# Twelve unread float32 products between the first modulation rows, and the first scores two steps of the key stream later

## The chip, the cores and the metric

One core of a Trainium2 chip runs the whole program. The metric is its time on the device in microseconds (us). The engines are named as in the profile: PE (TensorE, products), PEld (its weight loads), DVE (VectorE), ACT (ScalarE), POOL (GpSimd) and SP (SyncE, which here only issues transfers). Each engine works through its own instructions in a fixed order and waits on semaphores of the others.

## The reference

One inference step of a diffusion trunk of two layers on 512 latent tokens (a grid of 8 rows by 64 columns) and 128 prompt tokens, model width 1024, 16 heads of 64. Layer 0 is neighbourhood attention, layer 1 grouped-query attention; behind each stands a gated FFN with a width-3 convolution.

```
for l in range(2):
    shift, scale, gate (x2) = split(silu(cond) @ ada_w[l] + ada_b[l], 6)   # for latents and for prompt
    h = rmsnorm(x, g_pre[l]) * (1 + scale) + shift
    q, k, v = h @ w_qkv[l]
    x = x + gate * rmsnorm(attention(q, k, v, cached k, cached v) @ w_o[l], g_post[l])
    h = rmsnorm(x, g_ffn_pre[l]) * (1 + scale') + shift'
    u = conv3(h @ w_up[l]) + conv_b[l];  a, b = split(u, 2)
    x = x + gate' * rmsnorm((silu(a) * b) @ w_down[l], g_ffn_post[l])
```

Outputs are both token groups and the prompt's new keys and values.

## The kernel before, in words

Weights come as float32 and are split into a high part (`wh`, a cast on ACT) and the rest (`wl`, a subtraction on POOL or DVE); activations likewise. A large product is then three passes: high by high, low by high, high by low. All products are issued through `mm` and transposes through `turn`, which chain them so that PE runs them exactly in the order in which the program is written. The other engines' orders are set by a scheduler that models when things are ready; its order is fixed when the program is built, and each engine then runs its own in sequence. A transfer on SP's queue also waits its turn behind the one ahead.

*Start.* The tokens are loaded, normalised and transposed into `xT` (`tr`). For each of four pairs of 128-wide slices of the model width, `mod_load(i)` fetches four tiles `wf` of `ada_w` (seven buffers) and `mod_rows(i)` multiplies them with the conditioning vectors: for each tile four products of 32 output rows, which fill the four quarters of one bank named `row`. ACT copies the bank to `rs` (one buffer). `mod_cols(i)` turns it with four products by `sel`, two columns wide (`col`), and DVE and ACT then form the high and low part of `hT` for the two slices. The program order on PE is: rows 0, rows 1, columns 0, rows 2, columns 1, the value products `vp` of slices 0 and 1 for two token tiles (twelve), columns 2, the other `vp` of slices 0 and 1 and all of slices 2 and 3 (48), rows 3, and so on. `vb` holds five banks for the values of the five token tiles; each uses its columns 0 to 255.

*Attention of layer 0.* `stream()` yields the projections as 173 steps of six (keys and queries, `qk`) or up to nine products (values, `vp`): for each of eight pairs of heads eight steps for the queries and eight for the keys, and between them the values of heads 4 to 15. A step at the end of a half evicts its bank (`qs`; `kh` and `kl`), certain steps also issue the next weights' loads and splits, and the last item's steps 0, 2 and 4 issue those of the output projection (`m0.weights`, on POOL). `PRO` steps are drawn before the first head's scores:

```
        for _ in range(PRO):
            fill(1, 0)
        head = Head(0)
        for slot in range(4):
            head.scores(slot)
            fill()
```

Each of the four scores (`s`) is followed by a further step. Then come the heads: the letters of `ORDER` say what stands between the turns (`t`, which transpose the probabilities `p` into `tp`) of one head and the scores of the next: `f` draws a step, `a` a piece of `ada_work`, the later modulation rows (`ada`). The softmax of a score runs through DVE (minimum), ACT (exponential), DVE (reciprocal) and POOL (`p`); POOL also makes each head's table `tb` of biases from `tr`, which ACT's queue loads. With 19 steps ahead, 23 are drawn when head 0's loop begins and 165 when head 12's does; head 12 draws the last eight, and what it would draw beyond them is nothing. Then the weights and heads' outputs are split (`oh`, `ol`) and the output projection (`y`) starts.

*FFN.* `ux`, `uy`, `uz` are its up-products; on SP's queue loads of `in_ffn_w_up`, loads of `in_ada_w` for `ada_work`, stores of activations (`act`) and their reloads (`ain`) stand in one order.

Of the kernel before, what the change touches and what calls it, by code (L numbers as in the profile page):

```python
# [53 lines left out]
    "t0 s0 s1 f a f a f f t1 f f t2 a a f a f f a a s2 a f f a s3 f f a f f".split(),  # L54
    "t0 p0 s0 s1 f a f a f f t1 t2 a a f a f f a a v s2 p1 a f a s3 f p2 f".split(),
)
PRO = 19
PSTEP = (3, 5, 6, 6, 8, 9)
WU = 29
TP = 1  # L60
# [41 lines left out]
def hybrid_step(ctx: ExitStack, tc: tile.TileContext, A, O):  # L102
# [4 lines left out]
    def pe(ins):  # L107

        if pe_last[0] is not None:
            tc.add_manual_dep(ins.ins, pe_last[0], no_sync, reason="order")  # L110
        pe_last[0] = ins.ins.name

    def mm(*a, **k):
        pe(nc.tensor.matmul(*a, **k))  # L114
# [21 lines left out]
    ident = cst.tile([P, P], F32, name="ident")  # L136
# [317 lines left out]
    with ExitStack() as s:  # L454
# [3 lines left out]
        xts = []  # L458
# [51 lines left out]
        def mod_rows(i, ws):  # L510


            row = bk.get("row")
            for (n, h), w in ws.items():
                for j in range(4):
                    k = 4 * h + j
                    mm(row[32 * j : 32 * j + 32, 256 * n : 256 * n + 256], scolp[:, 2 * k : 2 * k + 32],
                       w[:, j, :], start=h == 0, stop=h == 1)
            rs = sp.tile([P, 512], F32, tag="rs", name="rs")
            nc.scalar.copy(rs, row)  # L520
            bk.put(row)
            return rs
# [41 lines left out]
        vb = [bk.get("vp") for _ in range(NT)]  # L564
# [13 lines left out]
        for t in range(NT):  # L578
            x_turn(t)
        rs = mod_rows(0, loads[0])  # L580
        for i in range(1, 3):
            nxt = mod_rows(i, loads[i])
            mod_cols(i - 1, rs)
            rs = nxt
        v_part(0, (0, 1))
        mod_cols(2, rs)
        v_part(0, (2, 3, 4))
        v_part(1, range(NT))
        rs = mod_rows(3, loads[3])
        v_part(2, (0, 1, 2))  # L590
        mod_cols(3, rs)
# [99 lines left out]
    with l_na:  # L691
# [261 lines left out]
        def fill(n=1, a=2):  # L953
            for _ in range(n):
                next(work, None)
            for _ in range(a):
                next(ada0, None)

        for _ in range(PRO):
            fill(1, 0)  # L960
# [620 lines left out]
    for hq in range(2):  # L1581
        for n, t in enumerate(((4, 0, 1, 2, 3), (0, 1, 2, 3, 4))[hq]):
# [3 lines left out]
            i = 5 * hq + n  # L1586
# [221 lines left out]
```

## Time and profile before

| | us |
|---|---|
| median of three runs | 1630.63 |
| lowest and highest | 1628.24, 1637.93 |
| the profiled execution's own time | 1631.72 |
| its span, first to last instruction | 1629.9 |
| PE busy in it | 1557.0 |

The mean granted clock of PE over the span is 0.986. In the profile a line such as `26.72 0.64 PE L114 MATMUL row<-wf,scolp 128*32 128x256 f32 x8 [0.87 <-DMA wf<-in_ada_w]` reads: at 26.72 us, lasting 0.64, eight records of products into `row` from `wf` and `scolp`, issued at line 114 (the helper `mm`; 117 is `turn`), before which PE sat idle for 0.87 until the load of `wf` landed. One float32 product leaves two records. Weights split into two parts leave one record for each product.

### The profile page before, as it was taken

Reading aid. Unit: us, or ns where it says so; the run is one execution under the profiler, and the core shown is the slowest. Engines: PE = TensorE matmul, PEld = TensorE weight load, DVE = VectorE, ACT = ScalarE, POOL = GpSimd, SP = SyncE. Lnnn points to the kernel's source line nnn. Section 1 sums busy time; section 2 is a strip of 40 time slices with the busy share of each in tenths; the row PEclk is TensorE's granted clock in tenths of the full one; section 3 lists DMA queues with packets and bytes.
Section 4 is the critical chain, followed back from the end, with each engine's and each line's share of the span. In section 5 each row is a group of like instructions: output and inputs, shape, how many; then the busy total and the mean of one; then the engine's idle time right before and its main releaser. Section 6 shows DMA issues by size and latency. Waiting matters only on the chain.

```text
span 1629.9 us, 26039 instructions
## 1 busy us (share of the span) xinstructions
PE 1557.0 (96%) x9709; PEld 1350.8 (83%) x9709; DVE 1011.8 (62%) x1645; ACT 858.0 (53%) x1641; POOL 723.0 (44%) x614
## 2 busy tenths in 40 slices
PE   5999999899999999999999997999999999999998
PEld 3888889778888888998887776777898999998886
DVE  3453534549866565775465877773787888885454
ACT  3464646545545454554444445763565656565433
POOL 1554545423253544544343355441524556563333
PEclk8999999999999999999999999999999999999999
DMA  9745553245466666348575110002635333338664
GB/s 286 184 138 143 137 143 73 63 135 176 147 199 214 196 204 207 103 161 299 197 235 178 60 39 14 1 1 101 220 114 187 117 103 109 107 115 285 209 210 140
DMA packets 193211, 242.42 MB, mean 149 GB/s; under 512 B 11100, under 2 KB 149564, under 8 KB 193084
## 3 DMA queue, kind: packets, MB, share of 16 engines
q1 hardware_dynamic: 182224, 233.13, 45.2%
q10 hardware_dynamic: 10860, 7.62, 2.7%
q8 instruction: 76, 1.25, 0.3%
q14 instruction: 51, 0.42, 0.1%
HBM read 214.38 MB, written 26.34 MB: 148 GB/s over the span
## 4 chain that ended last, share of the span: by engine, by line
PE 65%; DVE 12%; POOL 6%; DMA 6%; issue 5%; ACT 4%; SPq 1%; ACTq 0%; POOLq 0%; DVEq 0%
PE acc L114 18%; PE ux L114 10%; PE y L114 7%; PE qk L114 5%; PE uz L114 5%; PE s L114 4%; PE po L114 4%; PE tp L117 3%; PE vp L114 3%; DMA wr<-in_ada_w 3%; PE uy L114 3%; POOL wl L1099 2%; PE ada L114 2%; DVE t L1175 2%; DVE al L1099 1%
## 5 line engine op out<-in xcount | busy, mean ns | idle before, releaser
L167 POOL TENSOR_TENSOR wl<-wr,wh 128x1024 fp32r<-128x1024 f32 x75 | 183.7, 2452 | 267.1 <-ACT wh L165 260.6
L1099 POOL TENSOR_TENSOR wl<-wr,wh 128x1024 fp32r<-128x1024 f32 x80 | 194.6, 2451 | 55.5 <-ACT wh L1098 46.2
L114 PE MATMUL ux<-B,wh 128*128 128x322 f32 x832 | 201.9, 313 | 1.7 <-DVE B L220 1.6
L1175 DVE SCALAR_TENSOR_TENSOR t<-C,cw,t 128x644 f32<-128x644 f32 x176 | 156.5, 889 | 57.4 <-ACT t L1173 56.6
L114 PE MATMUL acc<-wh,alo 128*128 128x512 f32 x440 | 172.0, 391 | 0.0
L114 PE MATMUL acc<-wh,ahi 128*128 128x512 f32 x440 | 171.9, 391 | 0.0
L114 PE MATMUL acc<-wl,ahi 128*128 128x512 f32 x440 | 171.8, 391 | 0.0
L165 ACT CAST wh<-wr 128x1024 fp32r<-128x1024 f32 x140 | 145.3, 1048 | 32.9 <-DMA wr<-in_ffn_w_down 23.9
L114 PE MATMUL uz<-B,wh 128*128 128x322 f32 x640 | 158.5, 316 | 0.0
L114 PEld LDWEIGHTS ux<-B,wh 128*128 128x128 f32 x832 | 143.7, 189 | 9.4 <-issue 2.9
L1068 DVE TENSOR_TENSOR alo<-ain,ahi 128x384 fp32r<-128x384 f32 (+1 forms) x88 | 70.9, 815 | 95.7 <-ACT ahi L1066 95.4
L114 PE MATMUL ux<-B,wl 128*128 128x322 f32 x416 | 129.1, 310 | 0.0
L114 PE MATMUL qk<-hT,wh 128*128 128x384 f32 (+1 forms) x512 | 126.0, 319 | 0.3 <-DVE qs L776 0.2
L114 PEld LDWEIGHTS uz<-B,wh 128*128 128x128 f32 x640 | 111.8, 190 | 6.6 <-issue 3.7
L1099 POOL TENSOR_TENSOR vl<-wr,vh 128x1024 fp32r<-128x1024 f32 x38 | 96.8, 2547 | 36.4 <-ACT vh L1098 36.4
L1098 ACT CAST wh<-wr 128x1024 fp32r<-128x1024 f32 x88 | 89.6, 1050 | 33.1 <-DVE wr L1122 31.8
L1066 ACT CAST ahi<-ain 128x384 fp32r<-128x384 f32 (+1 forms) x88 | 40.2, 461 | 124.8 <-PE acc L114 91.7
L1173 ACT ACTIVATE t<-C,cw 128x644 f32<-128x644 f32 x88 | 78.7, 895 | 48.5 <-DVE C L1203 44.3
L114 PE MATMUL uz<-B,wl 128*128 128x322 f32 x320 | 100.2, 313 | 0.5 <-POOL wl L1099 0.4
L167 DVE TENSOR_TENSOR wl<-wr,wh 128x1024 fp32r<-128x1024 f32 x65 | 83.5, 1299 | 25.0 <-ACT wh L165 24.5
L114 PEld LDWEIGHTS acc<-wl,ahi 128*128 128x128 f32 x440 | 82.6, 188 | 18.0
L114 PEld LDWEIGHTS acc<-wh,ahi 128*128 128x128 f32 x440 | 82.6, 188 | 17.7
(249 smaller groups left out, 4009.4 us busy)
## 6 DMA issues: line engine op xcount, KB each, us to landing
wr<-in_ffn_w_up SPq DMA_DIRECT2D x88, 512.0 KB
wr<-in_ffn_w_down SPq DMA_DIRECT2D x88, 512.0 KB
wr<-in_ada_w SPq DMA_DIRECT2D x80, 512.0 KB
act<-act SPq DMA_DIRECT2D x44, 321.0 KB
wr<-in_na_w_qkv SPq DMA_DIRECT2D x24, 512.0 KB
mod<-modrow SPq DMA_DIRECT2D x20, 512.0 KB
ain<-act SPq DMA_DIRECT2D x44, 192.0 KB
wf<-in_ada_w SPq DMA_DIRECT2D x16, 512.0 KB
```

The source lines that it names most:

```text
L114: pe(nc.tensor.matmul(*a, **k))
L117: pe(nc.tensor.transpose(*a, **k))
L165: i = nc.scalar.copy(hi, raw)
L167: j = (low or nc.vector).tensor_sub(lo, raw, f32(hi))
L1066: nc.scalar.copy(hi[:, 0 : c1 - c0], ain[:, 0 : c1 - c0])
L1068: nc.vector.tensor_sub(lo[:, 0 : c1 - c0], ain[:, 0 : c1 - c0], f32(hi[:, 0 : c1 - c0]))
L1098: nc.scalar.copy(hl[0], src)
L1099: low.tensor_sub(hl[1], src, f32(hl[0]))
L1173: nc.scalar.activation(t, taps(0), AF.Identity, bias=cw[:, 3, n : n + 1], scale=cw[:, 1, n : n + 1])
L1175: nc.vector.scalar_tensor_tensor(t, taps(d), cw[:, w, n : n + 1], t, op0=ALU.mult, op1=ALU.add)
```

## The change

It does two things. In `mod_rows` for rows 0, 1 and 2 each tile's four products are followed by one float32 product of the identity with 256 columns of the first token tile, into columns 256 to 511 of the last value bank, which nothing reads. And `PRO` is 21: two more steps of the stream stand ahead of the first scores, and so all later steps stand two earlier against the heads; head 12 is left with six.

```
--- before.py
+++ after.py
@@ -54,7 +54,7 @@
     "t0 s0 s1 f a f a f f t1 f f t2 a a f a f f a a s2 a f f a s3 f f a f f".split(),
     "t0 p0 s0 s1 f a f a f f t1 t2 a a f a f f a a v s2 p1 a f a s3 f p2 f".split(),
 )
-PRO = 19
+PRO = 21
 PSTEP = (3, 5, 6, 6, 8, 9)
 WU = 29
 TP = 1
@@ -510,12 +510,15 @@
         def mod_rows(i, ws):
 
 
+
             row = bk.get("row")
             for (n, h), w in ws.items():
                 for j in range(4):
                     k = 4 * h + j
                     mm(row[32 * j : 32 * j + 32, 256 * n : 256 * n + 256], scolp[:, 2 * k : 2 * k + 32],
                        w[:, j, :], start=h == 0, stop=h == 1)
+                if i < 3:
+                    mm(vb[4][:, 256:512], ident, xts[0][:, 0:256], start=True, stop=True)
             rs = sp.tile([P, 512], F32, tag="rs", name="rs")
             nc.scalar.copy(rs, row)
             bk.put(row)
```

With the written order the scheduler's order changes too. On PE, around the first score of head 0 (`s`; `qk` are the stream's products, `tk` turns the prompt's keys of the first pair), before:

```order
L114 MATMUL qk<-hT_128,wh 128x256
L114 MATMUL s<-kh_740,qs_668 128x384
L114 MATMUL s<-kl_615,qs_668 128x384
L114 MATMUL qk<-hT_127,wh 128x256
L114 MATMUL qk<-hT_127,wl 128x256
L114 MATMUL qk<-hT_128,wh 128x256
L114 MATMUL qk<-hT_127,wh 128x256
L114 MATMUL qk<-hT_127,wl 128x256
L114 MATMUL qk<-hT_128,wh 128x256
L114 MATMUL s<-kh_740,qs_668 128x384
L114 MATMUL s<-kl_615,qs_668 128x384
L114 MATMUL qk<-hT_127,wh 128x384
```

and now:

```order
L114 MATMUL qk<-hT_127,wh 128x256
L114 MATMUL qk<-hT_127,wl 128x256
L114 MATMUL qk<-hT_128,wh 128x256
L114 MATMUL qk<-hT_127,wh 128x384
L114 MATMUL qk<-hT_127,wl 128x384
L114 MATMUL qk<-hT_128,wh 128x384
L114 MATMUL qk<-hT_127,wh 128x384
L114 MATMUL qk<-hT_127,wl 128x384
L114 MATMUL qk<-hT_128,wh 128x384
L117 MATMUL tk<-ident,kp 128x128
L114 MATMUL s<-kh_752,qs_680 128x384
L114 MATMUL s<-kl_627,qs_680 128x384
```

A step of 256 columns and one of 384, with the turn behind it, have come to stand ahead of the first score instead of behind the first and the second.

On POOL, at the end of the stream in head 12 (`p` are the softmax's last steps, `wl` splits of the output projection's weights, `tb` tables), before:

```order
L167 TENSOR_TENSOR wl<-wr,wh 128x1024
L826 TENSOR_TENSOR tb_611<-mask,tr 128x2x128
L869 TENSOR_SCALAR p<-p,rc 128x384 x2
L826 TENSOR_TENSOR tb_611<-mask,tr 128x256 x2
L869 TENSOR_SCALAR p<-p,rc 128x384 x2
L826 TENSOR_TENSOR tb_612<-mask,tr 128x2x128
L869 TENSOR_SCALAR p<-p,rc 128x384
L167 TENSOR_TENSOR wl<-wr,wh 128x1024
L869 TENSOR_SCALAR p<-p,rc 128x384
L167 TENSOR_TENSOR wl<-wr,wh 128x1024
L826 TENSOR_TENSOR tb_612<-mask,tr 128x256 x2
L869 TENSOR_SCALAR p<-p,rc 128x384 x2
```

and now:

```order
L872 TENSOR_SCALAR p<-p,rc 128x384 x2
L829 TENSOR_TENSOR tb_623<-mask,tr 128x2x128
L872 TENSOR_SCALAR p<-p,rc 128x384 x2
L829 TENSOR_TENSOR tb_623<-mask,tr 128x256 x2
L872 TENSOR_SCALAR p<-p,rc 128x384 x2
L829 TENSOR_TENSOR tb_624<-mask,tr 128x2x128
L167 TENSOR_TENSOR wl<-wr,wh 128x1024 x2
L872 TENSOR_SCALAR p<-p,rc 128x384
L167 TENSOR_TENSOR wl<-wr,wh 128x1024
L872 TENSOR_SCALAR p<-p,rc 128x384
L829 TENSOR_TENSOR tb_624<-mask,tr 128x256 x2
L872 TENSOR_SCALAR p<-p,rc 128x384 x2
```

The split of the first row before has moved behind the tables and the pairs of `p`, next to the following split: three splits now stand around the two single `p`, where two did. The same two `p` end both lists.

On SP, in the first steps of the FFN of layer 0, before:

```order
L1090 DMA wr<-in_ffn_w_up 128x8x128
L1214 DMA act_0_4379<-act 128x642
L277 DMA wr<-in_ada_w 128x1024
L1090 DMA wr<-in_ffn_w_up 128x8x128
L277 DMA wr<-in_ada_w 128x1024
L1064 DMA ain<-act_0_4379 128x384
L1214 DMA act_1_4380<-act 128x642
L277 DMA wr<-in_ada_w 128x1024
L1064 DMA ain<-act_1_4380 128x384
L277 DMA wr<-in_ada_w 128x1024 x2
```

and now:

```order
L1093 DMA wr<-in_ffn_w_up 128x8x128 x2
L277 DMA wr<-in_ada_w 128x1024 x2
L1217 DMA act_0_4391<-act 128x642
L277 DMA wr<-in_ada_w 128x1024
L1067 DMA ain<-act_0_4391 128x384
L277 DMA wr<-in_ada_w 128x1024
L1217 DMA act_1_4392<-act 128x642
L1093 DMA wr<-in_ffn_w_up 128x8x128
L277 DMA wr<-in_ada_w 128x1024
L1093 DMA wr<-in_ffn_w_up 128x8x128
```

Two loads of `in_ffn_w_up` and two of `in_ada_w` now go ahead of the first store of activations; before it was one of the former alone. After some 25 transfers both orders are the same again, and from there on to the end on every engine.

More of the change, by code (lines that the diff above doesn't have):

```diff
@@ L56 @@
 )
-PRO = 19
+PRO = 21
 PSTEP = (3, 5, 6, 6, 8, 9)
@@ L518, in mod_rows @@
                        w[:, j, :], start=h == 0, stop=h == 1)
+                if i < 3:
+                    mm(vb[4][:, 256:512], ident, xts[0][:, 0:256], start=True, stop=True)
             rs = sp.tile([P, 512], F32, tag="rs", name="rs")
```

## The prediction

> **What bounds the kernel now.** I read the page first, then TensorE's waits, then the stretches that the change touches.
>
> ```profile
> span 1629.9 us, 26039 instructions
> PE 1557.0 (96%) x9709; PEld 1350.8 (83%) x9709; DVE 1011.8 (62%) x1645; ACT 858.0 (53%) x1641; POOL 723.0 (44%) x614
> PE 65%; DVE 12%; POOL 6%; DMA 6%; issue 5%; ACT 4%; SPq 1%; ACTq 0%; POOLq 0%; DVEq 0%
> ```
>
> PE is busy for 96% of the span and holds 65% of the chain that ended last. Twelve more products can only cost what no wait hides, and moving two steps of the key stream removes no work. All that is to be won is idle time (1629.9 - 1557.0 = 73 us in all) and time at a lower clock. The waits say how little of that lies in reach:
>
> ```profile
> PE ada L114 <- DMA wr<-in_ada_w: 11.9, 6, 3.3
> PE row L114 <- DMA wf<-in_ada_w: 5.9, 7, 2.7
> PE tp L117 <- POOL p L869: 3.8, 1, 3.8
> PE s L114 <- ACT kh L749: 1.6, 1, 1.6
> ```
>
> The columns are total, times, longest. `row` (the modulation rows) and `s` (the first scores) are the places edited, `tp` and `ada` are further along the streams that move. Together they are 23 us, 1.4% of the span.
>
> The clock is the other part. This is the view of busy time by stretches, cut at the places where the granted clock changes (stretch, its length, busy of PE, PEld, DVE, ACT, POOL, then PEclk, DMA share and GB/s):
>
> ```profile
> 23.22:26.64 3.42, 2.34 (x40) 0.88 (x32) 0.00 (x0) 0.58 (x1) 0.00 (x0) 1.00 1.09 348
> 26.64:30.05 3.41, 2.26 (x24) 1.28 (x24) 0.16 (x2) 0.10 (x1) 0.00 (x0) 1.00 1.10 349
> 30.05:33.46 3.41, 0.88 (x8) 0.23 (x8) 1.60 (x5) 3.41 (x6) 1.21 (x1) 0.50 1.09 347
> 33.46:36.88 3.42, 2.36 (x20) 0.41 (x16) 3.35 (x5) 0.20 (x1) 1.15 (x1) 0.50 1.09 348
> 36.88:40.29 3.41, 3.29 (x18) 2.48 (x19) 0.60 (x4) 0.32 (x1) 0.00 (x0) 0.50 1.09 348
> 40.29:43.70 3.41, 3.41 (x19) 3.41 (x17) 0.55 (x1) 3.40 (x6) 1.41 (x1) 0.50 1.13 333
> 43.70:47.12 3.42, 3.42 (x17) 3.42 (x17) 2.90 (x9) 2.43 (x5) 0.94 (x1) 0.50 1.21 291
> 47.12:50.53 3.41, 3.41 (x31) 3.41 (x30) 3.41 (x5) 1.86 (x2) 2.53 (x1) 1.00 1.21 258
> 81.25:84.66 3.41, 1.62 (x10) 1.19 (x10) 1.51 (x4) 3.30 (x8) 0.54 (x1) 1.00 0.75 176
> 84.66:88.08 3.42, 3.42 (x14) 3.32 (x13) 1.44 (x5) 3.29 (x8) 2.66 (x2) 0.50 0.07 20
> ```
>
> The clock is 0.50 from 30.05 to 47.12 and again from 84.66 to 88.08. It falls behind a stretch with 1.62 us of work and behind one with 2.26, but not behind one with 2.34. It comes back behind a stretch full of wide products (43.70), not behind 2.36 us of work (33.46), nor behind the two stretches from 36.88 that look full. These contain `col`, products that move two columns only: 1.87 and 1.25 us of it, and 1.05 us in the stretch at 26.64. So `col` seems to count for little as activity.
>
> **Edit 1, the twelve products.** The rows around them, from the timeline of PE:
>
> ```profile
> 21.96 2.96 PE L114 MATMUL row<-wf,scolp 128*32 128x256 f32 x40
> 25.21 0.64 PE L114 MATMUL row<-wf,scolp 128*32 128x256 f32 x8 [0.29 <-DMA wf<-in_ada_w]
> ...
> 28.23 0.64 PE L114 MATMUL row<-wf,scolp 128*32 128x256 f32 x8 [0.88 <-DMA wf<-in_ada_w]
> 28.80 1.05 PE L114 MATMUL col<-sel,rs 128*128 128x2 f32 x8
> 32.58 1.08 PE L114 MATMUL row<-wf,scolp 128*32 128x256 f32 x8 [2.72 <-DMA wf<-in_ada_w]
> ...
> 37.00 1.08 PE L114 MATMUL row<-wf,scolp 128*32 128x256 f32 x8 [0.43 <-DMA wf<-in_ada_w]
> 38.01 1.87 PE L114 MATMUL col<-sel,rs 128*128 128x2 f32 x8
> ...
> 42.45 1.70 PE L114 MATMUL col<-sel,rs 128*128 128x2 f32 x8
> ...
> 51.24 1.93 PE L114 MATMUL row<-wf,scolp 128*32 128x256 f32 x32
> ```
>
> Eight records are one group of four `row` products on one loaded tile. No row shows a float32 product of 128 by 128 with 256 columns, so I bound it. Four groups back to back take 1.93 at full clock and one alone 0.64, so a group in a row takes (1.93 - 0.64) / 3 = 0.43. The four of a group write four quarters of the partitions, the new product all of them at once, with as many columns: 0.43 is the nearest row. From below, four `col` products with a full stationary tile take 1.05, 0.26 each; from above, a group alone, 0.64. Twelve cost 3.1 to 7.7 us, 5.2 by the value taken. At half clock I double it to 0.86.
>
> The cover is the 5.9 us that `row` waits for its loads. Rows 0 and 1: five products stand ahead of the second group of row 1, so PE gets there at 24.92 + 5 x 0.43 = 27.1, its load long landed, and three groups and products of 0.86 end at 29.6, not 28.87. The first `col` comes 0.8 later, inside the 2.72 that PE waits until 32.58 anyway; the loads are a stream at 348 GB/s that does not hurry. Row 2: its loads land 1.47 us apart ((37.00 - 32.58) / 3). At full clock group and product take 0.86 and fit; `col` starts at 37.00 + 0.86 = 37.9, as before (38.01). At half clock they take 1.72, and do not fit: with the first pair ending at 33.4 at full clock, the others run 33.99, 35.7, 37.4 to 39.1, and `col` starts 1.1 later.
>
> So the sign hangs on the clock. With the products, the stretch from 26.64 is full but for `col`, so I expect 1.00 up to 33.46. The stretch from 30.05 then holds 0.9 us of them and the end of `col`, less than the 1.62 that lost the clock at 84.66, so it falls at 33.46. The next stretch holds work from 33.99 on, 2.89 us. The trace has 2.36 as too little and 3.42 as enough; 2.89 lies half way. I take it as enough, narrowly: the added products fill the whole array, unlike `col`. Then 1.00 returns at 36.88 instead of 47.12. `col` takes 1.05 for 1.87 (-0.8), the twelve value products up to 42.45 half of their 2.6 (-1.3), the next `col` 1.05 for 1.70, of which I count 0.5: **-2.6 us**, and the vector work behind starts as much earlier. I go no further, since DVE is busy for all of 47.12 to 50.53. If 2.89 is not enough, the next stretch holds 39.1 - 36.9 = 2.3 and the one after that 2.6 besides `col`, which is less, and all stays slow until 47.12: the 1.1 above, rounded to **+1.2 us**. Bounds: -4.6 (all of PE's work from 38.01 to 47.12 at double speed) to +2.5 (three products of row 2 at the upper price, 1.28 for 0.86, on top of 1.2).
>
> The Trainium skill, "TensorE: Matmul & The Clock Gate", Part 1, says that the clock opens after at least one busy window of about 3.4 us of sustained work and closes after an idle one. The trace agrees on the length (3.41) and on opening behind a full stretch, but not on closing: 2.26 busy of 3.41 lost it. By the page's word "sustained", 2.89 would not open it, and the sum would be that of the first rival below.
>
> **Edit 2, the first scores two steps later.**
>
> ```profile
> 77.41 0.52 PE L114 MATMUL qk<-hT,wh 128*128 128x384 f32 x2
> ...
> 78.47 0.52 PE L114 MATMUL qk<-hT,wh 128*128 128x384 f32 x2
> ...
> 80.12 0.40 PE L114 MATMUL qk<-hT,wh 128*128 128x256 f32 x2
> ...
> 80.83 0.40 PE L114 MATMUL qk<-hT,wh 128*128 128x256 f32 x2
> 83.03 0.44 PE L114 MATMUL s<-kh,qs 128*128 128x384 f32 x1 [1.56 <-ACT kh L749]
> 83.70 0.41 PE L114 MATMUL s<-kl,qs 128*128 128x384 f32 x1 [0.23 <-DVE kl L750]
> ```
>
> Six products of a step take 0.71 (80.83 - 80.12) or 1.06 (78.47 - 77.41). One step of each now stands ahead of the first score: 1.8 us of work against 1.56 + 0.23 of waiting. The keys' parts come when they came, so I leave 0.4 of waiting for the low part: -1.4. With the gap gone, the stretch from 81.25 is nearly full and the clock should stay at 1.00: half of 3.42, -1.7. Against it: the softmax of the first head now has two steps less behind it before its turns, and the turn waits for the last `p`:
>
> ```profile
> 91.81 1.15 POOL L869 TENSOR_SCALAR p<-p,rc 128x384 f32<-128x384 f32 x2
> ...
> 93.09 0.60 PE L117 MATMUL tp<-ident,p 128*128 128x128 f32 x4
> ```
>
> `p` ends at 92.96, 0.13 ahead of the turn, so there is no slack. The moved steps also put their own work ahead of that softmax: four evictions of `qs` on ACT and DVE, and behind the turn of `kp` a copy and a store on ACT's queue. Their loads were issued before step 19 and do not move against the scores. I take +0.5. Sum **-2.6**, bounds -3.5 (all of gap and clock) to +0.5 (the 1.8 comes back in front of the turn with the slow stretch behind it, so that nothing is won, and the 0.5 is lost).
>
> **What is late next: the end of the stream.** The two steps are missing in head 12, which draws 6 steps instead of 8.
>
> ```profile
> 302.45 2.39 POOL L167 TENSOR_TENSOR wl<-wr,wh 128x1024 fp32r<-128x1024 f32 x1
> ...
> 306.56 2.35 POOL L167 TENSOR_TENSOR wl<-wr,wh 128x1024 fp32r<-128x1024 f32 x1 [1.16 <-ACT wh L165]
> ...
> 310.50 1.16 POOL L869 TENSOR_SCALAR p<-p,rc 128x384 f32<-128x384 f32 x2
> ```
>
> Here PE's only long wait of this phase ends: 3.8 in the waits, `tp` for `p`. POOL works off two splits (`wl`), a table and `p`; in the new order three splits stand there, one more at 2.4. PE arrives with 1.8 us less work behind the scores of the next head. At worst both add up, +4.2; if ACT's and POOL's work starts as much earlier as the steps do, nothing, or -0.5. POOL idles in places before it, so I take half: **+2.0**. SyncE's queue is reordered in the first steps of the next phase, the conv FFN: `ada_w` loads pass activation stores. PE waits there for them:
>
> ```profile
> 441.23 0.64 PE L114 MATMUL ada<-wr,scolp 128*32 128x256 f32 x8 [1.12 <-DMA wr<-in_ada_w]
> ...
> 462.87 0.64 PE L114 MATMUL ada<-wr,scolp 128*32 128x256 f32 x8 [1.76 <-DMA wr<-in_ada_w]
> ```
>
> and, from the view by stretches, the one behind the second wait:
>
> ```profile
> 463.53:466.94 3.41, 3.41 (x13) 3.41 (x14) 1.72 (x4) 1.58 (x3) 1.75 (x1) 0.50 0.63 155
> ```
>
> If both waits and the slow stretch behind the second go: -1.1 - 1.8 - 1.7 = -4.6. If a load now comes later, the longest such wait, 3.3, with a slow stretch: +5.0. I see no reason for a side and take 0. The order of what follows that phase's first steps is unchanged on every engine.
>
> **Sum.** The profiled execution took 1631.72 (span 1629.9). -2.6 - 2.6 + 2.0 + 0 = -3.2: **1628.5 us**. That execution is 1.1 above the median of the runs (1630.63; 1628.24 to 1637.93), less than they scatter; I do not correct for it.
>
> **The rivals.**
> - *The products do not open the clock* and only delay row 2. For it: 2.89 is unproven, the trace fails at 2.36. +1.2 for -2.6: 1631.72 + 1.2 - 2.6 + 2.0 = 1632.3. This is also what the change comes to if it doesn't do what it says. The Trainium skill's sentence on a sustained window, named above, gives this one.
> - *Slower: POOL's queue in head 12.* The third split comes straight ahead of the first `p` of head 13 and the filler is gone: +4.2, and one more stretch at half clock behind the longer wait, +1.7, together 5.9 for the 2.0 taken. It decides once this sum passes the gains: 5.2 with the forecast's clock (1631.72 - 5.2 + 5.9 = 1632.4), 1.4 with the first rival's (1636.2). I put it half way, 1634.3. For it: the new order of POOL's rows. Against it: POOL is busy for only 44% of the span, so its work can slide ahead.
> - *SyncE's order decides*: both `ada` waits go (1628.5 - 4.6 = 1623.9) or one of 3.3 comes (1633.5).
>
> **Chances and range.** Forecast 0.45, first rival 0.32, slower 0.15, SyncE 0.08. Range 1622 to 1637: the forecast without the +2.0 and with the `ada` waits gone is 1622, the slower case with a scatter of 1 is 1637. About 1% (16 us) is what a measurement of this kernel can tell from no change; no case comes near it. I leave 0.02 for faster and 0.03 for slower, 0.95 for within 1%.
>
> **What would show it.** Clock 1.00 up to 33.46 and from 36.88 on; PE's wait for `wf` down from 5.9 to under 3; no wait of `s` over 0.5 near 80 and no 0.50 behind it; the wait of `tp` for `p` near 305 grown from 3.8 to about 6; `ada` waits of similar sum. The forecast is wrong if the clock stays at 0.50 until 47, if that wait passes 7, or if the first turns wait for `p` by what the scores no longer wait.

## The result, and the profile after

The changed kernel took 1644.59 us (median of five runs, 1642.11 to 1645.37), the kernel before 1630.63 (the median of five as well) in the same session. The ratio is 1.0072 with a 95% interval of 1.0048 to 1.0095; it is an estimate over all the runs, and the two medians alone would give 1.0086. The change is slower by 0.7%, where 1628.5 was forecast and 1637 was the upper end. The profiled execution is the 1644.59 itself. Its page (the span, the busy time by engine):

```profile
span 1642.6 us, 26081 instructions
PE 1564.3 (95%) x9733; PEld 1353.4 (82%) x9733; DVE 1018.1 (62%) x1645; ACT 859.4 (52%) x1641; POOL 725.2 (44%) x614
```

PE is busy 7.3 us longer (1564.3 for 1557.0), and the rest of the 12.7 us of span is idle time. Its waits (total, times, longest):

```profile
PE tp L117 <- POOL p L872: 10.9, 4, 3.9
...
PE ada L114 <- DMA wr<-in_ada_w: 7.8, 5, 2.4
...
PE tp L117 <- DVE qs L779: 5.5, 3, 1.8
...
PE vp L114 <- DVE hT L547: 4.5, 4, 1.3
...
PE s L114 <- DVE qs L779: 2.1, 3, 0.8
...
PE row L114 <- DMA wf<-in_ada_w: 0.8, 1, 0.8
```

The edited waits are gone: `row` for `wf` is down from 5.9 to 0.8, and `s` for `kh` is no longer in the list. Four others have grown or are new. Where the loss stands can be read from the busy time up to the first product of the output projection (`y`, at 315.0 before and 333.7 after), first before and then after:

```profile
0.00:315.00 315.00, 288.96 (x2130) 249.99 (x2131) 134.03 (x362) 173.91 (x442) 148.90 (x158) 0.96 0.56 149
```

```profile
0.00:333.74 333.74, 295.05 (x2154) 251.73 (x2155) 141.42 (x366) 175.46 (x446) 151.98 (x158) 0.95 0.52 142
```

PE's idle time up to there grew from 26.0 to 38.7, by 12.7, and its busy time by 6.1, through the added products and through work at half clock. So at `y` the kernel is 18.7 late, more than at its end (12.7). Nearly all of the added idle time falls into six places:

| place | before | after | |
|---|---|---|---|
| `row` for `wf` | 5.9 | 0.8 | -5.1 |
| first scores | 1.8 | 0 | -1.8 |
| value products for `hT` | 2.1 | 4.5 | +2.4 |
| first turn of head 0 for `p` | 0 | 3.4 | +3.4 |
| heads 1, 5, 9 for `qs` | 0 | 7.6 | +7.6 |
| end of the stream | 4.2 | 9.7 | +5.5 |
| sum | | | +12.0 of 12.7 |

**The start.** The stretches of the changed kernel, cut where its granted clock changes (columns as in the forecast):

```profile
30.47:33.89 3.42, 2.47 (x27) 1.44 (x25) 0.91 (x4) 2.44 (x4) 0.14 (x1) 0.99 1.10 349
33.89:37.30 3.41, 3.41 (x20) 1.21 (x12) 3.16 (x3) 1.27 (x3) 2.21 (x1) 0.51 1.09 348
37.30:40.71 3.41, 3.41 (x31) 2.74 (x30) 1.64 (x6) 1.06 (x2) 0.00 (x0) 1.00 1.09 348
...
44.13:47.55 3.42, 0.94 (x6) 0.52 (x5) 3.39 (x8) 3.12 (x5) 0.24 (x1) 0.99 1.20 291
47.55:50.96 3.41, 3.41 (x16) 3.41 (x17) 3.41 (x4) 1.16 (x2) 3.23 (x1) 0.51 1.14 291
...
98.75:102.16 3.41, 3.41 (x21) 2.57 (x20) 2.20 (x8) 2.82 (x10) 0.62 (x2) 0.51 0.58 171
```

The clock does what was forecast: 1.00 to 33.89, one slow stretch, 1.00 again from 37.30 and not from 47.12. But the gain does not get past the vector work. PE, DVE and POOL around 42, in three fences:

```profile
40.93 0.95 PE L114 MATMUL col<-sel,rs 128*128 128x2 f32 x8
...
45.57 0.51 PE L114 MATMUL vp<-wh,hT 128*128 128x256 f32 x2 [1.21 <-DVE hT L547]
...
47.47 0.80 PE L114 MATMUL vp<-wh,hT 128*128 128x256 f32 x2 [1.28 <-DVE hT L547]
```

```profile
41.92 0.16 DVE L538 SCALAR_TENSOR_TENSOR gcol<-col,colb 128x4 f32<-128x4 f32 x1 [0.39 <-PE col L114]
42.00 0.15 DVE L540 TENSOR_TENSOR hcol<-col,colb 128x4 f32<-128x4 f32 x1
42.12 2.28 DVE L539 TENSOR_TENSOR gcol<-gcol,colb 128x4 f32<-128x4 f32 x1
44.32 0.34 DVE L546 TENSOR_SCALAR xT<-xT,gcol,hcol 128x128 f32<-128x128 f32 x1
```

```profile
41.96 2.41 POOL L167 TENSOR_TENSOR wl<-wr,wh 128x1024 fp32r<-128x1024 f32 x1 [5.86 <-ACT wh L165]
```

`col` comes at 40.93 instead of 42.45 and runs at full clock, so DVE's first `gcol`, which reads it, stands at 41.92 instead of 44.19, 2.3 earlier. The second `gcol`, four columns wide, then lasts 2.28 and ends at 44.40, when POOL's split ends (41.96 + 2.41 = 44.37). In the kernel before, the split ran from 42.29 to 44.64, and `gcol` came at its end:

```profile
44.38 0.27 DVE L536 TENSOR_TENSOR gcol<-gcol,colb 128x4 f32<-128x4 f32 x1
```

So the vector work behind it starts at 44.32 for 44.58: of 2.3 us, 0.3 are left, PE waits twice for `hT`, and behind a stretch with 0.94 of work the clock is 0.50 again from 47.55.

**The first turn.** The turn of head 0 waits for the last `p` (first PE, then POOL):

```profile
98.04 0.33 PE L117 MATMUL tp<-ident,p 128*128 128x128 f32 x1 [3.35 <-POOL p L872]
```

```profile
95.08 2.35 POOL L167 TENSOR_TENSOR wl<-wr,wh 128x1024 fp32r<-128x1024 f32 x1
97.40 0.59 POOL L872 TENSOR_SCALAR p<-p,rc 128x384 f32<-128x384 f32 x1
```

In the new order a split of weights stands ahead of that `p`; before, the split followed it (`p` from 91.81, `wl` at 94.64). The wait is twice what the scores saved, and the slow stretch has moved with it, from 84.66 to 98.75.

**Heads 1, 5 and 9.** In these heads the prompt's scores (`sp`) are issued. PE, and DVE's queue beside it, in head 1:

```profile
119.50 0.44 PE L114 MATMUL s<-kh,qs 128*128 128x384 f32 x1 [0.75 <-DVE qs L779]
...
123.00 0.63 PE L117 MATMUL tp<-ident,p 128*128 128x128 f32 x4 [1.82 <-DVE qs L779]
```

```profile
118.06 1.38 DVE L779 SCALAR_TENSOR_TENSOR qs<-qk,qs 64x256 fp32r<-64x256 f32 x3 [6.07 <-ACT qs L778]
119.47 0.42 DVE L627 TENSOR_REDUCE nmp<-sp 128x2 f32<-128x256 f32 x1
119.93 0.56 DVE L779 SCALAR_TENSOR_TENSOR qs<-qk,qs 64x384 fp32r<-64x384 f32 x1
120.52 0.42 DVE L627 TENSOR_REDUCE nmp<-sp 128x2 f32<-128x256 f32 x1
...
122.63 0.23 DVE L779 SCALAR_TENSOR_TENSOR qs<-qk,qs 64x64 fp32r<-64x64 f32 x1
```

A turn reads no `qs`: what it waits for is the bank, which the eviction of the queries has yet to empty. With the stream two steps further, that eviction stands among the prompt's reductions (`nmp`) and the next head's minimum in DVE's order, and its last piece ends at 122.86. Heads 5 and 9 show the same two waits (0.81 and 1.82, 0.55 and 1.82): 7.6 in all.

**The end of the stream** (PE's three long waits, two of the stretches there, then POOL and DVE):

```profile
320.15 0.33 PE L117 MATMUL tk<-ident,kp 128*128 128x128 f32 x1 [2.14 <-ACT kp L793]
324.93 0.48 PE L117 MATMUL tp<-ident,p 128*128 128x128 f32 x1 [2.97 <-POOL p L872]
329.33 0.47 PE L117 MATMUL tp<-ident,p 128*128 128x128 f32 x1 [3.92 <-POOL p L872]
```

```profile
317.20:320.61 3.41, 1.27 (x8) 0.94 (x7) 1.54 (x5) 3.36 (x10) 3.41 (x2) 0.99 0.14 47
320.61:324.03 3.42, 1.35 (x5) 0.66 (x3) 2.95 (x6) 3.08 (x8) 3.42 (x4) 0.50 0.75 262
```

```profile
316.18 4.68 POOL L167 TENSOR_TENSOR wl<-wr,wh 128x1024 fp32r<-128x1024 f32 x2
...
327.06 3.33 POOL L872 TENSOR_SCALAR p<-p,rc 128x384 f32<-128x384 f32 x2
```

```profile
326.30 1.87 DVE L167 TENSOR_TENSOR wl<-wr,wh 128x1024 fp32r<-128x1024 f32 x1
328.09 1.85 DVE L915 TENSOR_TENSOR ol<-of,oh 128x640 fp32r<-128x640 f32 x2
```

One wait of 3.8 and a short one have become four, 9.7 together with a last one of 0.65, and the clock is 0.50 for 17.1 us (five stretches from 320.61) instead of 6.8. Two splits now run one after the other ahead of the first of the last four `p`, and a third behind it. And the last two `p` take 3.33, where two took 1.16 in the kernel before (310.50 in the forecast's rows), while DVE works on a split and on `ol`: that is some 2.2 of the 5.5 that this place lost.

**Behind it** the kernel makes good 6.0 of the 18.7 us, 4.3 of them up to the first of the last products (`acc`) of the FFN of layer 0. Among PE's waits there, those of `ada` are shorter. Whose doing that is, the experiments below ask and do not settle.

### The profile page after: what moved, and what is told of

It is laid out like the page before. It is cut to its first block, busy times and chain, and to the rows that moved or that the text cites. A ratio compares the mean times of both kernels' runs of the same rounds, so it can differ in the third digit from the quotient of the medians.

```text
span 1642.6 us, 26081 instructions
## 1 busy us (share of the span) xinstructions
PE 1564.3 (95%) x9733; PEld 1353.4 (82%) x9733; DVE 1018.1 (62%) x1645; ACT 859.4 (52%) x1641; POOL 725.2 (44%) x614
## 4 chain that ended last, share of the span: by engine, by line
PE 72%; DVE 9%; POOL 6%; DMA 4%; ACT 4%; issue 4%; ACTq 0%; SPq 0%; POOLq 0%; DVEq 0%
PE acc L114 18%; PE ux L114 12%; PE y L114 7%; PE qk L114 6%; PE uz L114 5%; PE po L114 4%; PE s L114 4%; PE vp L114 4%; PE tp L117 3%; PE uy L114 3%; POOL wl L1102 2%; PE ada L114 2%; DMA wr<-in_ada_w 2%; PE gp L114 2%; DVE al L1102 1%
```

## The experiments

The first four rows separate the parts. The ratio is to the kernel before, run on the same chip in the same session. The changed kernel and the two steps alone ran five times, one step and the last splits on DVE four times, the moved prompt's scores six times, the others ten or twelve times; the intervals are as wide as that makes them.

| kernel | median us | ratio (95%) |
|---|---|---|
| changed kernel | 1644.59 | 1.0072 (1.0048 to 1.0095) |
| products alone | 1632.17 | 0.9994 (0.9975 to 1.0012) |
| two steps alone | 1647.81 | 1.0081 (1.0052 to 1.0110) |
| first two scores alone | 1627.12 | 0.9969 (0.9952 to 0.9985) |
| one step | 1649.19 | 1.0092 (1.0063 to 1.0122) |
| two steps, prompt's scores moved | 1638.61 | 1.0052 (1.0034 to 1.0070) |
| two steps, given back in head 11 | 1639.47 | 1.0044 (1.0025 to 1.0064) |
| two steps, last splits on DVE | 1643.60 | 1.0082 (1.0051 to 1.0114) |
| two steps, both mends | 1632.27 | 1.0016 (1.0001 to 1.0032) |
| products, one split on DVE | 1631.93 | 1.0007 (0.9994 to 1.0021) |
| first two scores and products | 1627.38 | 0.9975 (0.9958 to 0.9991) |
| the same, one split on DVE | 1627.76 | 0.9972 (0.9957 to 0.9988) |
| one product ahead of head 0 | 1629.37 | 0.9988 (0.9970 to 1.0006) |
| the same, first two scores | 1627.94 | 0.9979 (0.9963 to 0.9996) |

**Products alone** (the lines in `mod_rows`, `PRO = 19`).

> The twelve unread products alone, the stream drawn as before (PRO = 19). My theory after the first comparison: the products do bring the clock back near 37, but what PE gains up to 43 it then waits for the vector work behind hT, and falls to half clock again, so that at the first product of the stream it stands about where it did in the changed kernel (+3.2 us against before), while everything behind costs what it did before: 1631 to 1635 us. Rival A (the products are what makes the changed kernel slow, through a clock history that goes on into the later stages): 1640 or more. Rival B (the forecast's own sum for this part, -2.6): about 1628.

It is no change that can be told from noise: 0.9994. The interval goes down to 0.9975, so the time alone doesn't exclude the forecast's -2.6 either. At the first product of the stream it stands +0.58 against before, not +3.2 as the theory had it; the changed kernel's profiled execution had two further slow stretches from 61.20. Kernels that have the same instructions up to that point (before, and those below without the products) stand between -0.5 and +2.0 there in their profiles, so half a microsecond is nothing. The rest of the theory holds: the clock is back at 36.8, and PE waits 1.20 and 1.28 for `hT` as in the changed kernel. Its first rows give the price of a product among groups that wait for nothing (0.63 from 21.49 to 22.12, and 0.57 for a group):

```profile
20.92 0.64 PE L114 MATMUL row<-wf,scolp 128*32 128x256 f32 x8
21.49 0.70 PE L114 MATMUL vp<-x,ident 128*128 128x256 f32 x2
22.12 0.64 PE L114 MATMUL row<-wf,scolp 128*32 128x256 f32 x8
```

**Two steps alone** (`PRO = 21`, no products).

> The two steps alone (PRO = 21, no added products). Theory: the stream's later position against heads 1 to 12 costs most: three collisions of the query eviction with the prompt's scores in heads 1, 5 and 9 (about 2.6 us each), the longer starvation at the end of the stream with its slow clock (about +5 and +5), less some 5 that the conv FFN gives back: 1640 to 1643 us. Rival A (the products cost it): 1629 to 1632. Rival B (the forecast's sum for this part with the end of the stream, -0.6): about 1630.

1.0081: the whole loss, and somewhat more than I had from the trace; its interval overlaps with that of the changed kernel. Its profile has the same waits as the changed kernel's, in the same places (3.36 at the first turn, 7.6 for `qs`, 9.9 at the end).

**First two scores alone:** they come later, the stream does not move.

```
-PRO = 19
+PRO = 21
...
         for slot in range(4):
             head.scores(slot)
-            fill()
+            fill(int(slot > 1))
```

> PRO = 21, but no step is drawn behind the first two scores of head 0, so that 23 steps are drawn when its turns begin, as before: the first score stands two steps later, the second one, and every later step where it was. Theory (the shift of the whole stream costs, not the later first scores): 1628 to 1632 us, with no waits of s for qs in heads 1, 5 and 9 and a wait of tp for p of under 5 near 310. Rival (the later first scores themselves delay what follows): 1638 or more.

0.9969: faster than before (1627.12, a little under the 1628 to 1632 expected), and 18 us under the kernel that also moves the stream (1.0081 - 0.9969, 1.1%). So what costs is not that the first scores come later, but that the whole stream behind them stands elsewhere. Whether the 0.3% is won by the scores is asked at the end. Its POOL queue at the first turn, and PE's wait:

```profile
90.41 2.29 POOL L869 TENSOR_SCALAR p<-p,rc 128x384 f32<-128x384 f32 x4
92.64 2.40 POOL L167 TENSOR_TENSOR wl<-wr,wh 128x1024 fp32r<-128x1024 f32 x1
```

```profile
91.06 0.33 PE L117 MATMUL tp<-ident,p 128*128 128x128 f32 x1 [1.06 <-POOL p L869]
```

Here all four `p` stand ahead of the split, and the turn waits 1.06 and three times 0.23. The slow stretch near 84 is gone and none follows.

**One step** (`PRO = 20`, no products).

> One step later instead of two (PRO = 20, no added products). Theory (the phase of query evictions against the prompt's scores in heads 1, 5 and 9 decides, by where the half's last step falls): if the loss grows with the shift, about half of that of two steps, 1634 to 1638 us; if the collision needs the second step, 1629 to 1633 with only the longer wait at the end of the stream. Rival (the products cost it): 1629 to 1632, and no longer wait at the end.

Both forms of the theory were wrong in size: one step costs as much as two, 1.0092. The waits have moved on: in heads 1, 5 and 9 it is now a step of the stream that finds no bank, and again a turn:

```profile
112.56 0.36 PE L114 MATMUL qk<-hT,wh 128*128 128x256 f32 x1 [1.72 <-DVE qs L776]
...
116.00 1.09 PE L117 MATMUL tp<-ident,p 128*128 128x128 f32 x4 [2.13 <-DVE qs L776]
```

With the other two heads that is 11.6 us, more than the 7.6 of two steps, and the waits at the end of the stream are 8.4. The loss does not grow with the shift; it depends on which evictions meet.

**The two steps, with the prompt's scores at their old place in the stream** (of the letters of heads 1, 5 and 9).

```
-    "a f a f p0 t0 a s0 f s1 t1 a f t2 ...
+    "p0 a f a f t0 a s0 f s1 t1 a f t2 ...
```

> The two steps (PRO = 21, no products), with the prompt's scores of heads 1, 5 and 9 issued ahead of that head's first two steps instead of behind them, so that they stand at the same place of the stream as before. Theory (the prompt's scores meet the query evictions there): the six waits for qs, 7.6 us, are gone or under 1 us each head, the end of the stream stays as it was with two steps: 7 to 8 under the two steps alone, 1639 to 1641 us. Rival (the waits come from the turns' banks, which are still two steps off): the waits move but stay, 1645 to 1649.

1.0052, 0.3% or 4.7 us under the two steps alone. The waits in these heads are one each (1.34, 1.21, 0.66, at a turn of cached keys, `tk`), 3.2 for 7.6, and the end of the stream is as it was. So the theory holds for 4.4 of 7.6; the rest is the rival's, another bank that is still two steps off. (By time alone this mend and the next are at the edge of the noise, since each is a difference of two ratios with intervals of 0.2 to 0.3% to either side. What each takes away is read from the waits.)

**The two steps, given back in head 11.**

```
                 if step == "f":
+                    if h == 11 and i < 4:
+                        continue
```

> The two steps, given back in head 11, whose first two steps are not drawn, so that head 12 begins with 165 steps drawn as before. Theory: heads 1, 5 and 9 keep their waits for qs, the end of the stream is again one wait of 3.8 with 6.8 us at half clock: about 8 under the two steps alone, 1638 to 1641 us. Rival (the end of the stream is nothing by itself, the heads cost all): 1645 to 1648.

1.0044, 0.37% or 6.0 us under the two steps alone. The waits for `qs` are unchanged, the end of the stream is that of the kernel before:

```profile
324.21 1.04 PE L117 MATMUL tp<-ident,p 128*128 128x128 f32 x2 [3.78 <-POOL p L869]
```

**The two steps, with the last three splits on DVE.**

```
-                        m0.weights(0, OW[i], nc.gpsimd)
+                        m0.weights(0, OW[i])
```

> The two steps, with the three splits of the output projection's weights at the end of the stream on DVE instead of POOL. If POOL's queue starves the turns there (the forecast's slower rival), the waits of tp for p near 325 fall from 7.7 to under 3 and the time by 4 to 8: 1639 to 1644 us. Rival (too little PE work is left in head 12 whatever POOL does): the same waits on another engine, 1645 to 1649.

The median of its four runs falls into the theory's range, but against the kernel before its ratio is that of the two steps alone (1.0082 and 1.0081). The waits speak for the rival: 5.33 and 1.30 for `p`, 6.6 for 7.7. But POOL was not really relieved. Its rows, and the split that DVE works on beside the first:

```profile
314.62 1.88 POOL L869 TENSOR_SCALAR p<-p,rc 128x384 f32<-128x384 f32 x1 [1.85 <-PE qk L114]
...
321.92 3.98 POOL L869 TENSOR_SCALAR p<-p,rc 128x384 f32<-128x384 f32 x2
```

```profile
314.84 1.21 DVE L167 TENSOR_TENSOR wl<-wr,wh 128x1024 fp32r<-128x1024 f32 x1
```

One `p` takes 0.58 on an undisturbed POOL; here 1.88, and two take 3.98, while DVE works on a split and, beside the two, on `ol` (from 321.31 and 323.68) and another split (322.55). What would be left of the wait with POOL really free stays open.

**The two steps with both mends.**

> The two steps with both mends: the prompt's scores of heads 1, 5 and 9 at their old place in the stream, and the two steps given back in head 11. Theory (the two losses are separate and add): two steps alone 1.0081, less 0.0029 and 0.0037, so 1.001 to 1.003 of the kernel before, 1633 to 1636 us; what stays is the first turn's wait of 3.4 for p behind a split on POOL, with its slow stretch. Rival (what one mend saves, the other saves too): 1637 to 1640.

1.0016, within the forecast of 1.001 to 1.003 (the median, 1632.27, is a little under its 1633): the two losses add, as far as the noise lets one say (0.0029 and 0.0037 of 0.0081; the rival's 1637 lies at the interval's upper end). The two mends together are clear of the noise, 0.0065 under the two steps alone. The first turn's wait of 3.35 behind the split is still there.

**The products, with one split on DVE:** the one that POOL had at 41.96.

```
-            wv[i] = wsplit(rows(wqkv, 4 * i, 4, 2048, 256), 4, 256, nc.gpsimd)
+            wv[i] = wsplit(rows(wqkv, 4 * i, 4, 2048, 256), 4, 256, None if i else nc.gpsimd)
```

> The twelve products alone, with the split of the second half of the value weights on DVE (behind gcol in its order) instead of POOL; nothing else moves. Theory: with the products, DVE's small gcol at 42.1 lasts 2.28 us instead of 0.27, since POOL works on that split from 41.96 to 44.36, and this is where the earlier clock's 1.5 us go. Without POOL there, gcol takes under 0.4 and the split about 1.2 on DVE, so the last hT of that stage comes some 1 us earlier and PE's waits for hT near 45 and 47 (2.48 together) fall by about 1; the time stays within 1628 to 1633 us. Rival (gcol waits for something else, or the vector work is bound by its own sum): gcol stays near 2.3, or the waits do not fall.

DVE's rows of this kernel, and PE's two waits:

```profile
41.88 0.16 DVE L539 TENSOR_TENSOR gcol<-gcol,colb 128x4 f32<-128x4 f32 x1
41.96 1.23 DVE L167 TENSOR_TENSOR wl<-wr,wh 128x1024 fp32r<-128x1024 f32 x1
```

```profile
44.69 0.51 PE L114 MATMUL vp<-wh,hT 128*128 128x256 f32 x2 [0.56 <-DVE hT L547]
...
46.14 0.51 PE L114 MATMUL vp<-wh,hT 128*128 128x256 f32 x2 [0.83 <-DVE hT L547]
```

`gcol` is back to 0.16, the split takes 1.23, and the two waits fall from 2.48 to 1.39, as the theory had it. It was POOL's split that held the DVE. The time does not show it: 1.0007.

**Both later first scores and products, without and with that split on DVE.**

> The twelve products, and the first two scores later without moving the stream (PRO = 21, no step behind the first two scores). Theory (the products are worth nothing, the local move 3 to 5 us): as the local move alone, 1625 to 1629 us. Rival (the two parts disturb each other, as the wait for hT moves): 1631 or more.

> The candidate for a version better than both: products, first two scores later without moving the stream, and the split of the second half of the value weights on DVE. Theory: 0.5 to 1.5 us under the version without that last edit, 1625 to 1628 us. Rival (DVE has no room for the split): 1628 or more.

0.9975 and 0.9972. Neither differs from the later first scores alone (0.9969) by more than the noise: the products show no gain beside them either. All three beat both kernels; the simplest of them is the first two scores alone.

**Is it the first scores that win the 0.3%?** In the profile of that kernel only 0.9 us of its lead are there at the first `y`, and 6.9 behind the FFN. (The two profiled executions are 8.1 apart, more than the 5 by which the runs differ.) It also has the changed kernel's order of SyncE's queue in the FFN, since the scheduler's plan moves with the first scores; so have all kernels above with `PRO` of 20 or 21, while the products alone, with either engine for the split, keep the old order. Two kernels were meant to take this apart. Both issue one unread product ahead of head 0, which turns the ring of banks by one and gives both the same queue of SyncE, in which two loads of `ada_w` stand elsewhere than before:

```
+        _z = bk.get("zz")
+        mm(_z[:, 0:128], ident, ident, start=True, stop=True)
+        bk.put(_z)
         head = Head(0)
```

One has the scores as before, the other the first two scores later.

> One unread float32 product of 128 by 128 with 128 columns ahead of head 0, into a bank of its own, which turns the ring of banks by one; the scores as before. It is the partner of the next kernel: from the FFN on, the two have the same order on every engine, and SyncE's queue is the same throughout, one ada_w load away from that of before. I expect 1631 to 1634 us, as before within 0.2%.

> The same product, with the first two scores later (PRO = 21, no step behind the first two scores). The two differ on PE, DVE, ACT and POOL only around the first scores and in some orders in head 1. Theory A (the later first scores are themselves worth the 0.3% that the kernel with them alone won): 4 to 5 us under the partner. Theory B (what won is the order of SyncE's queue in the FFN of layer 0, which the later first scores change in the scheduler's plan and which here is the same in both; the gap itself is worth about 1, as at the first product of the output projection in the profiles): 0 to 2 us under the partner.

The first of them came out at 1629.37 (0.9988), under the 1631 to 1634 expected. The means of their twelve runs each differ by 1.35 us (1630.22 and 1628.87; 95% interval -1.3 to +4.0). That is in theory B's range, but the interval holds no difference at all and ends where theory A's 4 begins, so it doesn't decide. The profiles don't either. At the first `y` they differ by 1.2, but at the first product of the stream, up to which both have the same instructions, they already stand 1.9 apart (66.77 and 64.89). And the second kernel does not close the gap at the first scores, it moves it: its third score waits 1.31 for `kl` at 85.62, where its partner's first waits 1.18 and 0.23. So what wins the 0.3% stays open: the later first scores, the order of transfers in the FFN, or both. No kernel has the old scores with the new order.

## Why the prediction was wrong

**Edit 1, -2.6: the clock was right, the sum was not.** The clock fell at 33.89 and was back at 37.30, where 33.46 and 36.88 were forecast. The price was too low: a group and its product take 1.20 in a full row, 0.57 and 0.63, not 0.43 each, so the twelve cost 7.6, next to the upper bound of 7.7. So at row 2 the slow stretch was full (3.41) rather than 2.89, and the disputed number was not tried: that 2.89 is enough stays unproven, and that the clock came back is in part luck. (The ground given for it doesn't hold as it stands. `col` too has a full stationary tile, 128*128 in its rows; it differs in the columns that it moves, 2 for 256.) The Trainium skill, "TensorE: Matmul & The Clock Gate", Part 1, asks for a sustained window before the clock opens. The stretch behind which it opened here was full, 3.41 of 3.41, so the trace agrees. The Trainium skill, "TensorE: Matmul & The Clock Gate", Part 1, also lets the clock close after an idle window. Here it closed behind stretches with 2.47 and 0.94 of 3.41 busy, so the trace does not agree.

The step that failed is the last one, "the vector work behind starts as much earlier". The first `gcol` did stand 2.3 earlier, close to the 2.6, but the work behind the second started 0.3 earlier, since POOL's split held that one. The Trainium skill has this rule, in "SBUF — State Buffer", section "Who interferes with whom": a DVE instruction with two inputs in SBUF and a GpSimd instruction that reads SBUF share a port, and the second to issue is blocked until the first is done. The trace agrees: `gcol`, with two such inputs, ends 0.03 after the split, while `hcol`, which reads `col` from its bank, took 0.15 at 42.00 beside it. By its time the edit shows no gain (0.9994, an interval from -4 to +2 us), and in the trace 0.3 of its 2.6 get past the vector work.

**Edit 2, -2.6: two steps of it failed.** The gap did close and the slow stretch behind it went. But "I take +0.5" for the turn that waits for `p` was 3.35, with a slow stretch of its own. I had seen that `p` had no slack, and had not looked at the new order of POOL at that place, where the split went ahead of it. This is the last sign that the forecast named against itself: the first turns wait for what the scores no longer wait. Without the shift, too, PE's wait changes its place: 1.8 is gone at the scores, and the turns wait 1.8 for their four `p`. The slow stretch is gone, and at the first `y` that profile is 0.9 ahead, not 2.6.

The second failure is the larger. The sum had an entry for the beginning of the stream and one for its end, and none for the twelve heads between. That "all later steps stand two earlier against the heads" moves every eviction of the stream against every softmax, and in three heads the prompt's scores make that tight: 7.6 us of waits, 4.4 of them taken back by moving the prompt's scores alone, for 0.29% (by time at the edge of the noise).

**The end of the stream, +2.0.** The place and its sign were right, the size was not. 4.2 was given as the worst, and half of it taken on the ground that POOL idles in places before it; the rival adds that POOL is busy for only 44% of the span. The waits grew by 5.5, and the clock was slow for 10 us more. The share of busy time was the wrong row: POOL has hardly a gap from 317.20 to 330.39 (3.41 and 3.42 in the two stretches shown). It did idle before, for 4.27 us up to 315.34, but it waited there for a load of `tr`, and the splits stand behind that table in its order. The 4.2 also left out that PE waits 2.14 for `kp` from ACT, and that POOL's last two `p` take 3.33 for 1.16 beside DVE. Given back in head 11, this term measured 6.0 (0.37%, with the noise named above).

**SyncE's order, 0.** Open. From the first `y` to the first `acc` of that FFN the changed kernel makes good 4.3 us against the profile of before. The ten kernels with the new order make good 1.7 to 7.6 there, 4.5 in the mean; of the two others with the old order one makes good 5.8 and one loses 2.4. The last pair, which has one order, makes good 2.0 and 5.6. So single profiles scatter by several us at this place, and a gain by the new order is possible, but not shown.

**The rivals.** The slower one was POOL's queue in head 12, at 1634.3 with 0.15; its mechanism measured 0.37 of the 0.81% that the two steps lost. The larger parts, heads 1, 5 and 9 and the first turn, stood in no rival, so the range ended at 1637. With 0.7% the result lies within the 1% to which 0.95 was given, but 1% was too coarse a bound for what a measurement here can tell: the interval of 1.0048 to 1.0095 is clear of no change.

## What to carry to other kernels

A step that moves a producer's stream by a little moves it against every consumer up to its end: look at the order of each recurring place (here one head in four), not only at the first and the last. To close one gap, move the instructions at the gap and give the shift back at once (0.9969 here, for 1.0081 with the shift kept). And before crediting a faster engine, read what the next engine's short instructions stand beside: here a gain of 2.3 us stopped at one instruction four columns wide.

## What the hardware showed that I had not expected

- DVE and POOL held each other here for whole instructions, both ways: `gcol` took 2.28 for 0.16 beside a POOL split, POOL's `p` 1.88 for 0.58 beside a DVE split, and two `p` 3.33 for 1.16 beside a DVE split and `ol`. So it matters which two meet: one split moved to DVE freed `gcol`, three moved to DVE did not free POOL.
- A float32 product of 128 by 128 with 256 columns takes 0.63 us at full clock in a row with groups of `row` products (21.49 to 22.12), its two records 0.70 together.
- The clock fell behind a stretch that was 72% busy (2.47 of 3.41, of which 0.9 is `col`), and not behind one of 69% without `col` (2.34, from 23.22 before). So the busy share alone does not decide it.
- The stretches of the clock lie on a grid of 3.41 us ((88.08 - 23.22) / 19 in the forecast's rows), which stands elsewhere against the program in each execution (slow from 30.05 before, from 33.89 after). Kernels with equal instructions up to the stream's first product reach it up to 2.5 us apart, about as much as was forecast for either edit at the start.
